# Splitting the first load of an add-GELU kernel by partitions: 16 rows first, then 112

## The chip, the cores and the metric

The kernel runs on one core of one Trainium2 chip. The metric is the device time of one execution in microseconds (us), taken as the median of several runs. "Span" is the length of a profiled execution; it is some 1.8 us shorter than the device time of the same run.

Some words: an *issue* is the instruction by which SyncE asks for a transfer. The core's 16 DMA engines carry the transfer as *packets*, each one row of a load or store, 8 to 32 KB in these two kernels. A transfer has *landed* when the last engine has signalled it. In the views DVE is VectorE, ACT is ScalarE, POOL is GpSimd and SP or SPq is SyncE.

## The reference

```python
# x, y: float32 [1024, 4096]
z = x + y
out = 0.5 * z * (1 + tanh(sqrt(2 / pi) * (z + 0.044715 * z ** 3)))   # float32
```

Two arrays of 16.8 MB come in and one goes out: 50.33 MB in all, for a handful of elementwise operations.

## The kernel before

Every array is seen as 128 partitions of 32768 elements; partition p holds eight neighbouring rows of 4096. x and y come in five column pieces each, the sum is made in place in the tile `z`, and `z` is stored again in five pieces. All loads and stores go through one queue (SyncE). The first two loads are moved ahead of the opening barrier.

```python
YS = 8192; CH = 1024; PS = 4
loads  = [2048, 6144, 8192, 8192, 8192]      # columns per partition
stores = [8192, 8192, 8192, 4096, 4096]
...
def load_x(i):
    a, b = lr[i]
    nc.sync.dma_start(out=zt[:, a:b], in_=xv[:, a:b])

def load_y(i):
    a, b = lr[i]
    s, o = divmod(a, YS)
    if o == 0:
        yt[s] = pool_y.tile([P, YS], fp32, tag="y", name=f"y{s}")     # two buffers
    nc.sync.dma_start(out=yt[s][:, o : o + b - a], in_=yv[:, a:b])
...
# per piece of 1024 columns: add (GpSimd; VectorE for the first), Square (ScalarE),
# scalar_tensor_tensor (VectorE), Sigmoid (ScalarE), multiply (VectorE)
...
sp = []
for i in range(len(loads)):
    sp += [(load_x, i), (load_y, i)]
sp += [(store, i) for i in range(len(stores))]
...
begin_early(nc, 2)      # the first two loads are issued ahead of the opening barrier
```

Of the kernel before, what the change touches and what calls it, by code (L numbers as in the profile page):

```python
# [1 line left out]

# [1 line left out]

# [4 lines left out]


def begin_early(nc, count):


    blocks = nc.main_func.blocks
    head, body = blocks[0], blocks[1]
    SP = mybir.EngineType.SP
    queue = [i for i in body.instructions if i.engine == SP]
    moved = [i for i in queue if isinstance(i, mybir.InstDMACopy)][:count]
    assert not any(i.sync_info and i.sync_info.on_wait for i in moved)
    at = next(k for k, i in enumerate(head.instructions) if i.engine == SP and isinstance(i, mybir.InstDrain))  # L20
    for k, i in enumerate(moved):
        body.instructions.remove(i)
        head.instructions.insert(at + k, i)


@with_exitstack
def kernel(
    ctx: ExitStack,
    tc: tile.TileContext,
    x: bass.AP,  # L30
    y: bass.AP,
    out: bass.AP,
):








    nc = tc.nc
    P = nc.NUM_PARTITIONS
    fp32 = mybir.dt.float32
    act = mybir.ActivationFunctionType
    alu = mybir.AluOpType

    N, D = x.shape
    assert N % P == 0
    TOT = N // P * D  # L50
    xv, yv, ov = (a.rearrange("(p n) d -> p (n d)", p=P) for a in (x, y, out))

    c1 = 2.0 * math.sqrt(2.0 / math.pi)
    root = math.sqrt(c1 * 0.044715)

    YS = 8192
    CH = 1024
    PS = 4
    loads = [2048, 6144, 8192, 8192, 8192]
    stores = [8192, 8192, 8192, 4096, 4096]  # L60

    def ranges(sizes):
        ends = [sum(sizes[: i + 1]) for i in range(len(sizes))]
        assert ends[-1] == TOT
        return [(e - f, e) for e, f in zip(ends, sizes)]

    lr, sr, cr = ranges(loads), ranges(stores), ranges([CH] * (TOT // CH))
    C = len(cr)
    by_pool = set(range(1, C))

    def over(rs, lo, hi):
        return [i for i, (a, b) in enumerate(rs) if a < hi and b > lo]

    pool_sb = ctx.enter_context(tc.tile_pool(name="xz", bufs=1))
    pool_y = ctx.enter_context(tc.tile_pool(name="y", bufs=2))
    pool_w = ctx.enter_context(
        tc.tile_pool(name="w", bufs=PS, space=bass.MemoryType.PSUM)
    )

    zt = pool_sb.tile([P, TOT], fp32, tag="z", name="z")  # L80
    yt, wt = {}, {}

    def load_x(i):
        a, b = lr[i]
        nc.sync.dma_start(out=zt[:, a:b], in_=xv[:, a:b])  # L85

    def load_y(i):
        a, b = lr[i]
        s, o = divmod(a, YS)
        if o == 0:  # L90
            yt[s] = pool_y.tile([P, YS], fp32, tag="y", name=f"y{s}")
        nc.sync.dma_start(out=yt[s][:, o : o + b - a], in_=yv[:, a:b])  # L92

    def store(i):
        a, b = sr[i]
        nc.sync.dma_start(out=ov[:, a:b], in_=zt[:, a:b])

    def add(c):
        a, b = cr[c]
        s, o = divmod(a, YS)  # L100
        eng = nc.gpsimd if c in by_pool else nc.vector
        eng.tensor_add(out=zt[:, a:b], in0=zt[:, a:b], in1=yt[s][:, o : o + b - a])  # L102

    def sq(c):
        a, b = cr[c]
        wt[c] = pool_w.tile([P, CH], fp32, tag="w", name=f"w{c}")
        nc.scalar.activation(  # L107
            out=wt[c], in_=zt[:, a:b], func=act.Square, scale=root
        )

    def stt(c):
        a, b = cr[c]
        nc.vector.scalar_tensor_tensor(  # L113
            out=wt[c], in0=wt[c], scalar=c1, in1=zt[:, a:b], op0=alu.add, op1=alu.mult
        )

    def sig(c):
        nc.scalar.activation(out=wt[c], in_=wt[c], func=act.Sigmoid)  # L118

    def mul(c):  # L120
        a, b = cr[c]
        nc.vector.tensor_mul(out=zt[:, a:b], in0=wt[c], in1=zt[:, a:b])  # L122
# [6 lines that stand above are left out]
    pool = [(add, c) for c in range(C) if c in by_pool]  # L129
    dve, acts = [], []  # L130
    for i in range(-3, C + 1):
        if 0 <= i < C:
            dve.append((stt, i))
            acts.append((sig, i))
        if 0 <= i - 1 < C:
            dve.append((mul, i - 1))
        if 0 <= i + 3 < C and i + 3 not in by_pool:
            dve.append((add, i + 3))
        if 0 <= i + 2 < C:
            acts.append((sq, i + 2))  # L140

    needs = {
        load_x: lambda i: [],
        load_y: lambda i: [
            (add, c)
            for c in over(cr, lr[i][0] - 2 * YS, lr[i][0] - YS)
            if lr[i][0] % YS == 0
        ],
        add: lambda c: [(f, i) for i in over(lr, *cr[c]) for f in (load_x, load_y)],
        sq: lambda c: [(add, c)] + ([(mul, c - PS)] if c >= PS else []),  # L150
        stt: lambda c: [(sq, c)],
        sig: lambda c: [(stt, c)],
        mul: lambda c: [(sig, c)],
        store: lambda i: [(mul, c) for c in over(cr, *sr[i])],
    }
    queues = [sp, pool, acts, dve]
    done = set()
    with tc.manual_schedule():
        one = pool_sb.tile([P, 1], fp32, tag="one", name="one")
        nc.vector.memset(one, 0.0)  # L160
        nc.scalar.activation(out=one, in_=one, func=act.Sigmoid)  # L161
        while any(queues):
            moved = False
            for q in queues:
                while q and all(n in done for n in needs[q[0][0]](q[0][1])):
                    fn, arg = q.pop(0)
                    fn(arg)
                    done.add((fn, arg))
                    moved = True
                    if q is not sp:  # L170
                        break
            assert moved, [q[:1] for q in queues]

    ctx.close()
    tc.close()
    tc.compile()
    begin_early(nc, 2)


# [1 line left out]
_INS = ['x', 'y']  # L181
_OUTS = [((1024, 4096), 'float32')]


# [23 lines left out]
```

## Time and profile before

| | before |
|---|---|
| device time, median of the first 3 runs | 122.65 us |
| profiled span | 121.2 us |
| VectorE / ScalarE / GpSimd busy | 62% / 53% / 60% |
| share of the 16 DMA engines' time in the load and store queue | 97.8% |
| moved | 50.33 MB |

How to read it: no compute engine is near full, and the DMA engines are. The kernel is one stream of loads and stores, so the questions are when the stream starts, whether it ever slows, and when it ends. Three lines of the table of stretches (stretch, length, busy time of DVE, ACT and POOL with instruction counts, clock, DMA share, GB/s), which the argument after the prediction needs; the prediction shows more of this table:

```profile
3.00:6.00 3.00, 0.00 (x0) 0.00 (x0) 0.00 (x0) 1.00 1.00 421
6.00:9.00 3.00, 1.22 (x1) 0.27 (x1) 1.48 (x1) 1.00 1.14 489
70.00:82.00 12.00, 12.00 (x12) 9.72 (x10) 10.31 (x6) 1.00 1.00 404
```

The last line is the one to remember: in that stretch the stream runs at 404 GB/s and not at the 430 or so of its neighbours.

### The profile page before, as it was taken

What the parts mean: (1) busy time and instruction counts of PE and PEld (TensorE: products, weight loads), DVE (VectorE), ACT (ScalarE), POOL (GpSimd) and SP (SyncE); (2) the same over time, 40 slices, a digit from 0 to 9 for tenths busy, and PEclk for the clock granted to TensorE, in tenths of its full rate; (3) what the DMA queues carried; (4) which work ended last, traced back from release to release, by engine and by line L of the source; (5) the groups of instructions that cost most, each with busy time, mean ns of one, the idle gap of its engine ahead of it and who ended that gap; (6) DMA issues with size and microseconds to landing.
All of it is one profiled execution on the core that took longest, in us unless ns stands there. A gap on an engine that the chain in (4) does not pass through costs nothing.

```text
span 121.2 us, 248 instructions
## 1 busy us (share of the span) xinstructions
DVE 75.5 (62%) x66; ACT 63.8 (53%) x66; POOL 73.0 (60%) x35
## 2 busy tenths in 40 slices
DVE  0044700059999019999997999994999999400000
ACT  4016200078875047888858878874878878000000
POOL 0056000699980299999889999949999990000000
DMA  6999999999999989898989898998999999989992
GB/s 197 417 468 422 471 406 433 476 389 476 389 476 389 476 379 487 357 508 357 508 346 519 346 519 346 346 487 381 479 389 476 389 476 389 487 379 411 433 433 108
DMA packets 2162, 50.35 MB, mean 416 GB/s; under 512 B 240, under 2 KB 240, under 8 KB 240
## 3 DMA queue, kind: packets, MB, share of 16 engines
q1 hardware_dynamic: 2160, 50.33, 97.8%
q14 instruction: 2, 0.02, 0.0%
HBM read 33.55 MB, written 16.78 MB: 415 GB/s over the span
## 4 chain that ended last, share of the span: by engine, by line
DMA 49%; POOL 17%; DVE 16%; SPq 1%; ACT 1%; issue 0%; POOLq 0%
DMA y<-in_y_dram 49%; POOL z L102 17%; DVE z L122 8%; DVE w L113 8%; ACT w L107 1%; SPq L85 1%; SPq L92 1%; POOLq L102 0%
## 5 line engine op out<-in xcount | busy, mean ns | idle before, releaser
L102 POOL TENSOR_TENSOR z<-z,y 128x1024 f32<-128x1024 f32 x31 | 72.8, 2388 | 26.5 <-DMA y<-in_y_dram 26.5
L113 DVE SCALAR_TENSOR_TENSOR w<-w,z 128x1024 f32<-128x1024 f32 x32 | 39.4, 1232 | 21.4 <-ACT w L107 21.4
L107 ACT ACTIVATE w<-z 128x1024 f32<-128x1024 f32 x32 | 32.9, 1028 | 37.7 <-POOL z L102 31.7
L122 DVE TENSOR_TENSOR z<-w,z 128x1024 f32<-128x1024 f32 x32 | 38.8, 1214 | 0.0
L118 ACT ACTIVATE w<-w 128x1024 f32<-128x1024 f32 x32 | 31.4, 981 | 0.4 <-DVE w L113 0.4
L102 DVE TENSOR_TENSOR z<-z,y 128x1024 f32<-128x1024 f32 x1 | 1.2, 1224 | 6.1 <-DMA y<-in_y_dram 6.1
L161 ACT ACT_TABLE_LOAD x1 | 1.3, 1283 | 1.3 <-PEq L192 1.3
L160 DVE MEMSET one<- 128x1 f32 x1 | 0.1, 59 | 1.3 <-PEq L192 1.3
L192 POOL MEMSET const-float32-0.0<- 128x1 f32 x1 | 0.1, 99 | 0.2 <-issue 0.2
L161 ACT ACTIVATE one<-one 128x1 f32<-128x1 f32 x1 | 0.2, 203 | 0.0
L192 POOL MEMSET const-bfloat16-1.0<- 128x1 bf16 x1 | 0.1, 102 | 0.0
L192 POOL MEMSET const-uint8-127<- 128x1 uint8 x1 | 0.1, 102 | 0.0
L192 POOL MEMSET const-float32-1.0<- 128x1 f32 x1 | 0.1, 99 | 0.0
## 6 DMA issues: line engine op xcount, KB each, us to landing
z<-in_x_dram SPq DMA_DIRECT2D x3, 4096.0 KB, 34.2
y<-in_y_dram SPq DMA_DIRECT2D x3, 4096.0 KB, 24.8
out_dram<-z SPq DMA_DIRECT2D x3, 4096.0 KB, 30.8
out_dram<-z SPq DMA_DIRECT2D x2, 2048.0 KB, 17.5
z<-in_x_dram SPq DMA_DIRECT2D x1, 3072.0 KB, 13.4
y<-in_y_dram SPq DMA_DIRECT2D x1, 3072.0 KB, 20.4
z<-in_x_dram SPq DMA_DIRECT2D x1, 1024.0 KB, 4.9
y<-in_y_dram SPq DMA_DIRECT2D x1, 1024.0 KB, 6.9
```

Of the source, the lines that this page charges most:

```text
L85: nc.sync.dma_start(out=zt[:, a:b], in_=xv[:, a:b])
L92: nc.sync.dma_start(out=yt[s][:, o : o + b - a], in_=yv[:, a:b])
L102: eng.tensor_add(out=zt[:, a:b], in0=zt[:, a:b], in1=yt[s][:, o : o + b - a])
L107: nc.scalar.activation(out=wt[c], in_=zt[:, a:b], func=act.Square, scale=root)
L113: nc.vector.scalar_tensor_tensor(out=wt[c], in0=wt[c], scalar=c1, in1=zt[:, a:b], op0=alu.add, op1=alu.mult)
L118: nc.scalar.activation(out=wt[c], in_=wt[c], func=act.Sigmoid)
L122: nc.vector.tensor_mul(out=zt[:, a:b], in0=wt[c], in1=zt[:, a:b])
L160: nc.vector.memset(one, 0.0)
L161: nc.scalar.activation(out=one, in_=one, func=act.Sigmoid)
L192: nc = _bacc.Bacc("TRN2", target_bir_lowering=False, num_devices=1)
```

## The change

The intent, as I read the edit, is that a small first load gets its data moving earlier, while the rest of the first megabyte follows right behind.

```diff
     def load_x(i):
         a, b = lr[i]
-        nc.sync.dma_start(out=zt[:, a:b], in_=xv[:, a:b])
+        cut = [0, 16, P] if i == 0 else [0, P]
+        for f, e in zip(cut, cut[1:]):
+            nc.sync.dma_start(out=zt[f:e, a:b], in_=xv[f:e, a:b])
 ...
-    begin_early(nc, 2)
+    begin_early(nc, 3)
```

## The prediction

The forecast's sum stands as it was made: 0.01 us for the semaphore packets, -0.15 for an earlier start, and two terms of +0.3, one for a slow load of 16 rows and one for slow packets in the load of 112 rows. That is +0.46 us, weighed down by hand to about +0.3, so 122.95 us. Where the two terms of +0.3 came from is cut. So are rivals 2 and 3, in which the cut by rows costs more, or much more, than the sum has; their chances (45% and 7%) stand in the text.

> **What bounds the kernel now.** I read four views in this order: the page's busy shares and slices, to see which resource is never idle; the table of stretches, to see when that resource starts and stops; the timeline of the first microseconds, because that is where the change sits; and the page's DMA issues with the DMA queue's waits, to see whether the transfers ever run dry later.
>
> The page first (part 1, the DMA rows of part 2, part 3):
>
> ```profile
> DVE 75.5 (62%) x66; ACT 63.8 (53%) x66; POOL 73.0 (60%) x35
> ...
> DMA  6999999999999989898989898998999999989992
> GB/s 197 417 468 422 471 406 433 476 389 476 389 476 389 476 379 487 357 508 357 508 346 519 346 519 346 346 487 381 479 389 476 389 476 389 487 379 411 433 433 108
> ...
> q1 hardware_dynamic: 2160, 50.33, 97.8%
> ```
>
> No compute engine is busy above 62%, while the 16 DMA engines are at eight or nine tenths in every slice but the first and the last, and their one hardware queue takes 97.8% of their time. The kernel is a single stream of 50.33 MB (two inputs in, one output out). Only the first slice (6) and the last (2) are not full.
>
> The table of stretches puts numbers on it. The columns are the stretch, its length, the busy time of DVE, ACT and POOL with their instructions, the TensorE clock, the DMA share and GB/s:
>
> ```profile
> 0.00:1.00 1.00, 0.00 (x0) 0.00 (x0) 0.20 (x4) 1.00 0.00 0
> 1.00:2.00 1.00, 0.06 (x1) 0.74 (x1) 0.00 (x0) 1.00 1.07 156
> 2.00:3.00 1.00, 0.00 (x0) 0.74 (x2) 0.00 (x0) 1.00 0.93 393
> 2.00:60.00 58.00, 33.74 (x30) 28.97 (x31) 35.73 (x15) 1.00 1.01 432
> 60.00:119.00 59.00, 41.72 (x37) 34.05 (x35) 37.08 (x17) 1.00 1.00 426
> ```
>
> For 1.0 us nothing moves; for the next the engines count as busy but deliver 156 GB/s; from 2.0 to 119.0 us they run at 426 to 432 GB/s. The span of 121.2 us is thus about 2.0 (start) + 117.2 (stream) + 2.0 (last write, its landing and the end). A transfer of 1 MB costs 2.4 us of stream at 432 GB/s, and what shifts the stream's first full packet shifts the end by the same amount.
>
> The timeline of the start:
>
> ```profile
> 0.00 0.38 SPq L85 DMA_DIRECT2D z<-in_x_dram  x1
> ...
> 0.43 0.42 SPq L92 DMA_DIRECT2D y<-in_y_dram  x1
> 1.26 1.28 ACT L161 ACT_TABLE_LOAD   x1 [1.26 <-PEq L192]
> 1.26 0.33 SPq L85 DMA_DIRECT2D z<-in_x_dram  x1
> ```
>
> The first issue takes 0.38 us and starts at zero. The packet records of the trace have the first 8192-byte packet at 1.01 us, so 0.63 us after that issue ended; the 16 engines take up their first packet between 1.01 and 1.41 us. Joining packets end to start, I get 16 clean chains. Thirteen engines hold their first packet for 0.89 to 1.25 us; the other three do two packets in that time. All 16 reach the steady 0.306 us per 8192 bytes (26.8 GB/s an engine) between 2.0 and 2.4 us. So about 0.7 us per engine is a cold start. By the same chains the engines write their last packets' semaphores between 118.95 and 119.52 us, except one at 119.88: two 8 KB instruction fetches (at 83.9 and 86.5 us, 0.309 us each) went through the engines as well, and I take it that this one did them. So the end follows one engine's phase, not the mean.
>
> Last, the queue:
>
> ```profile
> z<-in_x_dram SPq DMA_DIRECT2D x1, 1024.0 KB, 4.9
> y<-in_y_dram SPq DMA_DIRECT2D x1, 1024.0 KB, 6.9
> ```
>
> The first x lands at 4.9 us, the first y 6.9 us after its own issue at 0.43; the third load is issued at 1.26, long before the engines need it. The issue times and landings further on never leave the queue empty: the last store is issued at 104.4 us while the one before it lands at 115.4. The page's chain that ended last (DMA 49%, POOL 17%, DVE 16%) follows semaphores into the compute engines, but these are 11 us ahead at the end; I set it aside.
>
> [...]
>
> **The change part by part.** It removes one 128-row load of 1 MB and adds a 16-row load (128 KB) and a 112-row load (896 KB) of the same bytes, all before the opening barrier; nothing moves on DVE, ACT or POOL (their instruction lists have the same order and count).
>
> Extra issue: one more of about 0.4 us (rows of 0.38 and 0.42). The first y is issued near 0.85 instead of 0.43, still over 3 us before its packets are due at about 4.3. The barrier and the third load move from 1.26 to at most 1.7; packets of that load are due near 6.8. Table load (1.28 us) and first compute (7.48) have more slack still. On the path: 0.
>
> Extra semaphore packets: one per engine, 9 ns in the records. On the path: +0.01 us.
>
> Earlier start: if the issue's time follows its descriptors, a 16-row issue ends before 0.38 and the first packets come that much earlier. Issues of 1, 3 and 4 MB, with the same row count, take 0.33 to 0.66 us, so bytes hardly matter and rows are untried. My estimate is a gain of 0.0 to 0.3 us, middle 0.15.
>
> [...]
>
> Sum: 0.01 - 0.15 + 0.3 + 0.3[...] gives about +0.3 us: 122.65 + 0.3 = 122.95.
>
> **The rivals.** (1) Earlier start wins[...]: 122.3 to 122.6. For it: the cold start wastes 0.7 us per engine with an idle queue ahead. Against: the first packets end at 2.0 to 2.4 us whether they began at 1.01 or 1.41[...]. [...] (4) It is hidden: since the stream is bound from 2.0 us on, nothing changes: 122.6 to 122.7.
>
> **Range and chances.** Rivals 1 and 4 together some 45%, 2 some 45%, 3 some 7%. That puts the middle at 122.95, and 8 in 10 between 122.2 and 124.4. Slower by over 2% is above 125.1: rival 3 with the far edge of 2, 0.08. Faster by over 2% needs 2.45 us less, more than the whole start: 0.01. Within 2%: 0.91.
>
> **What would show it.** First packet's start: under 1.0 us proves the earlier start. [...] I am wrong altogether if the stream later has gaps, or if either part runs on fewer than 16 engines.

## The result, and the profile after

The changed kernel took 123.13 us (median of 6 runs, 123.03 to 123.39), the kernel before 122.67 us in the same rounds (6 runs, 122.49 to 123.08). The ratio is 1.0038 with a 95% interval of 1.0019 to 1.0057: slower by 0.4%, and within 2%. Ratios here are the mean time of one kernel's fast runs over the mean of the other's fast runs of the same rounds, so they differ a little from the ratio of the medians.

The SyncE timeline of the changed kernel, start (columns: start and duration in us, engine, line, what):

```profile
0.00 0.86 SPq L88 DMA_DIRECT2D z<-in_x_dram  x2
0.90 0.43 SPq L95 DMA_DIRECT2D y<-in_y_dram  x1
1.74 0.35 SPq L88 DMA_DIRECT2D z<-in_x_dram  x1
```

The two halves of the first x are one merged line here; the records behind it have the 16-row issue at 0.00 for 0.39 us and the 112-row issue from 0.445 for 0.42 us. So the small issue was no shorter than the 128-row one (0.38 us), and the bulk of the data was asked for 0.445 us later. The first packet started at 1.03 us (1.01 before).

The changed kernel's DMA issues (KB each, us from issue to landing):

```profile
y<-in_y_dram SPq DMA_DIRECT2D x1, 1024.0 KB, 7.4
z<-in_x_dram SPq DMA_DIRECT2D x1, 896.0 KB, 5.6
z<-in_x_dram SPq DMA_DIRECT2D x1, 128.0 KB, 3.0
```

The small load landed 3.0 us after its issue. The 896 KB needed 5.6 us from its own issue, more than the 4.9 us that the whole megabyte took before.

The changed kernel's table of stretches, with the same columns as before:

```profile
1.00:2.00 1.00, 0.06 (x1) 0.27 (x1) 0.00 (x0) 1.00 1.26 246
2.00:3.00 1.00, 0.00 (x0) 1.00 (x1) 0.00 (x0) 1.00 0.65 238
3.00:6.00 3.00, 0.00 (x0) 0.22 (x2) 0.00 (x0) 1.00 0.98 322
6.00:9.00 3.00, 0.55 (x1) 0.00 (x0) 0.51 (x1) 1.00 1.13 478
70.00:82.00 12.00, 12.00 (x11) 10.16 (x11) 11.04 (x6) 1.00 1.02 437
```

Against before: up to 3 us the engines had moved 484 KB (246 + 238) instead of 549 KB (156 + 393). That is 65 KB, or 0.15 us at 432 GB/s. From 3 to 6 us they ran at 322 instead of 421 GB/s: 99 GB/s for 3 us is 297 KB, or 0.69 us. From 6 to 9 us another 0.08 us (489 against 478). Together 0.92 us. And then, at 70 to 82 us, the changed kernel was *faster*: 437 against 404 GB/s, which is 33 x 12 = 396 KB, or 0.92 us. That the two figures are equal is luck: this view counts every packet whole, so the edges of a stretch are uncertain, most of all at 70 and 82 us, where each engine carries 32 KB packets. With each packet's bytes spread over its time, the records give 404 and 432 GB/s there, or 0.76 us.

How the delay runs through the kernel is seen where GpSimd begins on a newly landed y. GpSimd's timeline, before:

```profile
60.99 18.52 POOL L102 TENSOR_TENSOR z<-z,y 128x1024 f32<-128x1024 f32 x8 [0.93 <-DMA y<-in_y_dram]
81.20 4.65 POOL L102 TENSOR_TENSOR z<-z,y 128x1024 f32<-128x1024 f32 x2 [1.69 <-DMA y<-in_y_dram]
```

and after:

```profile
61.86 18.54 POOL L105 TENSOR_TENSOR z<-z,y 128x1024 f32<-128x1024 f32 x8 [0.85 <-DMA y<-in_y_dram]
81.36 4.65 POOL L105 TENSOR_TENSOR z<-z,y 128x1024 f32<-128x1024 f32 x2 [0.96 <-DMA y<-in_y_dram]
```

At the last y but one the changed kernel is 0.87 us late, at the last y only 0.16 us. VectorE's first sum, before and after:

```profile
7.48 1.22 DVE L102 TENSOR_TENSOR z<-z,y 128x1024 f32<-128x1024 f32 x1 [6.08 <-DMA y<-in_y_dram]
8.45 1.23 DVE L105 TENSOR_TENSOR z<-z,y 128x1024 f32<-128x1024 f32 x1 [6.59 <-DMA y<-in_y_dram]
```

It starts 0.97 us late. So a delay of nearly 1 us is made in the first 9 us, carried for 50 us to within 0.1 us, and then mostly lost, because something holds up the kernel *before* near 77 us and does not hold up the changed one.

### The profile page after: what moved, and what is told of

It reads as the page before. It is cut to its first block, busy times and chain, and to the rows that moved or that the text cites. A ratio compares the mean times of both kernels' runs of the same rounds, so it can differ in the third digit from the quotient of the medians.

```text
span 121.2 us, 249 instructions
## 1 busy us (share of the span) xinstructions
DVE 75.6 (62%) x66; ACT 63.8 (53%) x66; POOL 73.1 (60%) x35
## 4 chain that ended last, share of the span: by engine, by line
DMA 49%; DVE 16%; POOL 16%; issue 2%; SPq 1%; ACT 1%; POOLq 0%
DMA y<-in_y_dram 49%; POOL z L105 16%; DVE z L125 8%; DVE w L116 8%; ACT w L110 1%; SPq L88 1%; SPq L95 1%; POOLq L105 0%
## 6 DMA issues: line engine op xcount, KB each, us to landing
y<-in_y_dram SPq DMA_DIRECT2D x3, 4096.0 KB, 24.8
```

## The experiments

Twelve runs were made, two of them of the same two kernels again, and all gave right results. "Late" below is the start of the first sum on VectorE, which waits for the first x and y: 7.48 us in the first profile of before. Passages of the expectations are cut as well, and marked, where they named a cause that no run shows. What stands right behind a cut, with no theory named, was expected if a cut by rows by itself makes a load slow, unless the text here says otherwise.

### Both kernels again

No edit. The aim was to learn which of the two differences above return.

> The kernel before, unchanged, to see how much two of its profiles differ. The profile of before holds a single stall in which packets took up to 0.54 us per 8 KB between 75 and 80 us (0.78 us per engine); the profile of after has none. Theory A (the stall is a chance event): the time ratio is 1.000 within 0.2%, and this profile has no such stall or has it elsewhere; then all landings of y4 are near 80.3 us instead of 81.06. Theory B (the stall belongs to the kernel before): it is there again at 75 to 80 us.

> The changed kernel again. Ratio to before 1.003 to 1.006 in both theories. If the start alone decides (loss seen in the profile at the landing of the first y: 8.33 against 7.38 us, 0.95 us), the whole loss must reach the end: about +0.9 us without a stall in before, so 1.007. If the stall is a chance event that the changed kernel has as well in other runs, the mean difference stays under that, near 0.5 us (1.004).

Measured: before again 122.54 us (ratio to its own rounds 1.0001, interval 0.9986 to 1.0016); after again 123.20 us against 122.59 us, ratio 1.0053 (1.0038 to 1.0068). Both profiles repeat. The first, of before:

```profile
3.00:6.00 3.00, 0.00 (x0) 0.00 (x0) 0.00 (x0) 1.00 1.02 429
70.00:82.00 12.00, 12.00 (x12) 9.71 (x10) 10.18 (x6) 1.00 0.98 393
```

and the second, of after:

```profile
3.00:6.00 3.00, 0.00 (x0) 0.22 (x2) 0.00 (x0) 1.00 1.00 309
70.00:82.00 12.00, 12.00 (x12) 10.16 (x12) 11.05 (x6) 1.00 1.00 429
```

The slow start (309 against 429 GB/s from 3 to 6 us) is again the changed kernel's, and the slow stretch at 70 to 82 us (393 against 429) is again the old one's. In this pair the first sum is 1.32 us late (8.60 against 7.28). The stall belongs to before in both profiles, and to after in none. Two profiles of each are few, but the table of all 14 profiles further down sorts by kernel too, eight with the stall and six without, so the chance theory falls.

### The same bytes, cut by columns

```diff
-        nc.sync.dma_start(out=zt[:, a:b], in_=xv[:, a:b])
+        cut = [0, 256, 2048] if i == 0 else [0, b - a]
+        for f, e in zip(cut, cut[1:]):
+            nc.sync.dma_start(out=zt[:, a + f : a + e], in_=xv[:, a + f : a + e])
...
-    begin_early(nc, 2)
+    begin_early(nc, 3)
```

> Same number of loads and the same bytes in the first one (128 KB), but cut by columns: 128 partitions x 256 elements, then 128 x 1792. [...]nothing is lost, packets of the second part take the usual time for their 7 KB (0.27 us), the first y lands at 7.3 to 7.5 us, time within 0.1 us of before. Extra-issue theory (what costs is one more issue of 0.39 + 0.05 us ahead of the bulk of the data, or the second part's cold start): the first y lands 0.4 to 0.9 us later than 7.38 as in after, time +0.3 to +0.5 us.

Measured: 122.84 us against 122.59 us, ratio 1.0026 (1.0001 to 1.0051). The table of stretches:

```profile
1.00:2.00 1.00, 0.06 (x1) 0.27 (x1) 0.00 (x0) 1.00 1.17 245
2.00:3.00 1.00, 0.00 (x0) 1.00 (x1) 0.00 (x0) 1.00 0.72 251
3.00:6.00 3.00, 0.00 (x0) 0.21 (x2) 0.00 (x0) 1.00 1.02 427
```

From 2 to 3 us this kernel is as slow as the changed one (251 and 238 GB/s): that part does not depend on how the load is cut. From 3 to 6 us it is as fast as before (427). The first sum starts at 7.65 us, 0.17 to 0.37 us late. So each of the two theories, slow rows and the extra issue, holds one share of the loss: some 0.2 to 0.3 us belong to a small piece issued ahead of the bulk, and the rest, the slow stretch from 3 to 6 us, belongs to the cut by rows. Within the first share, the later issue of the bulk and a slow start of the second piece are not told apart. One more issue is not enough by itself: the needless load further down also puts one ahead of the first x, but of 0.5 MB, and loses nothing by 3 us (188 + 381 = 569 KB against 549 of before):

```profile
1.00:2.00 1.00, 0.06 (x1) 0.28 (x1) 0.00 (x0) 1.00 0.90 188
2.00:3.00 1.00, 0.00 (x0) 1.00 (x1) 0.00 (x0) 1.00 0.98 381
```

The first share of the column cut is near the noise of this run (one of its six runs took 123.58 us).

### The 16/112 cut in the middle of the stream, and its control

The same cut on the third x (4 MB), some 20 us behind the start; and that same load cut by columns.

```diff
-        nc.sync.dma_start(out=zt[:, a:b], in_=xv[:, a:b])
+        cut = [0, 16, 128] if i == 2 else [0, P]
+        for f, e in zip(cut, cut[1:]):
+            nc.sync.dma_start(out=zt[f:e, a:b], in_=xv[f:e, a:b])
```

```diff
-        nc.sync.dma_start(out=zt[:, a:b], in_=xv[:, a:b])
+        cut = [0, 1024, 8192] if i == 2 else [0, b - a]
+        for f, e in zip(cut, cut[1:]):
+            nc.sync.dma_start(out=zt[:, a + f : a + e], in_=xv[:, a + f : a + e])
```

> The first loads are whole again; instead the third load of x (4 MB, in the middle of the stream, no cold start) is cut into 16 and 112 partitions. [...]the loss of the change's load times four, since rows are 32 KB and not 8[...]; I expect +2 to +8 us (1.02 to 1.07). [...]Extra-issue or cold-start theory: no loss, under 0.05 us.

> Control to the 16/112 split of the 4 MB load in the middle: the same load is cut by columns at full width, 128 x 1024 and 128 x 7168 (the same 512 KB first). [...]+0.0 us, within 0.2%, and packets at 0.304 us per 8 KB between 20 and 42 us. If an additional load as such costs: +1 us or more.

Measured: rows 131.44 us (ratio 1.0726, 1.0705 to 1.0746), 8.85 us more; columns 122.41 us (0.9983, 0.9967 to 1.0000). The stretch 25 to 42 us, in which most of the 112-row part runs, first with rows, then with columns:

```profile
25.00:42.00 17.00, 13.90 (x12) 11.66 (x12) 11.74 (x6) 1.00 0.96 260
```

```profile
25.00:42.00 17.00, 13.91 (x12) 11.25 (x12) 11.39 (x6) 1.00 1.01 435
```

The same number of loads and the same bytes: 260 against 435 GB/s. The cut by rows cost 8.85 us, the cut by columns nothing. (The stretch takes in some full-width packets behind the 112 rows; those rows alone hold each engine for 14.9 us in the packet records, which is 245 GB/s.) The 8.85 us are a little over the 2 to 8 us that I expected. In the packet records all 16 engines slow down alike, to 1.8 to 2.7 us for a 32 KB row, against 1.215 us for a row of a full-width load.

### Sixteen rows at a time

```diff
-        nc.sync.dma_start(out=zt[:, a:b], in_=xv[:, a:b])
+        cut = [0, 16, 32, 48, 64, 80, 96, 112, 128] if i == 2 else [0, P]
+        for f, e in zip(cut, cut[1:]):
+            nc.sync.dma_start(out=zt[f:e, a:b], in_=xv[f:e, a:b])
```

> The 4 MB load of the middle as eight loads of 16 partitions each, to measure the rate of a 16-row load by itself. [...]the 4.19 MB take 38.8 us instead of 9.7, so +29 us, if loads queue strictly[...]. [...]+0.1 us.

The first figure takes 16 rows to run at a quarter of the stream's rate, which was an assumption of mine; the second is for rows that do not matter.

Measured: 147.41 us (one run), 24.8 us more. The table of stretches:

```profile
26.00:52.00 26.00, 13.91 (x12) 11.57 (x12) 11.44 (x5) 1.00 1.01 122
```

Eight loads of 16 neighbouring rows in a row run at 122 GB/s, steadily, with all 16 engines counted as busy. A 32 KB packet takes 4.30 us on its engine, so each 8 KB takes 1.075 us instead of 0.304. 4.19 MB at 122 GB/s are 34.4 us instead of 9.7, so 24.7 us more; the time shows 24.8.

Now the middle split can be added up. 0.52 MB at 122 GB/s take 4.3 us and 3.67 MB at 260 GB/s take 14.1 us, 18.4 us in all instead of 9.7: +8.7, measured +8.85. The sum fits the time a little too well: where GpSimd begins on the last y but one, this kernel is 9.6 us late (70.62 against 60.99), and at the last y 8.9 (90.10 against 81.20), because it has no stall either. A quarter of 8.7 to 9.6, for rows of 8 KB, is 2.2 to 2.4 us: by this estimate that is what the changed kernel's cut would cost with nothing to hide it.

What makes such rows slow is not shown. I had put it down to the side of the on-chip memory, which was an assumption. But every cut by rows here also changes which rows of x or y in DRAM the 16 engines read at the same time, and no run separates the two sides.

### The 16/112 cut on the first y, and a 64/64 cut on the first x

The first tells whether the start hides a part: here the cut rows come when the stream already runs.

```diff
-        nc.sync.dma_start(out=yt[s][:, o : o + b - a], in_=yv[:, a:b])
+        cut = [0, 16, 128] if i == 0 else [0, P]
+        for f, e in zip(cut, cut[1:]):
+            nc.sync.dma_start(out=yt[s][f:e, o : o + b - a], in_=yv[f:e, a:b])
...
-    begin_early(nc, 2)
+    begin_early(nc, 3)
```

The second halves the first x:

```diff
-        nc.sync.dma_start(out=zt[:, a:b], in_=xv[:, a:b])
+        cut = [0, 64, 128] if i == 0 else [0, P]
+        for f, e in zip(cut, cut[1:]):
+            nc.sync.dma_start(out=zt[f:e, a:b], in_=xv[f:e, a:b])
...
-    begin_early(nc, 2)
+    begin_early(nc, 3)
```

> The first x is whole again; the first y (1 MB) is cut into 16 and 112 partitions[...]. From the runs so far: 16 rows of 8 KB take 1.075 us on each engine (the eightfold run) instead of 0.306, so +0.77; seven rows each at the 1.7-fold pace of the middle split, 7 x 0.306 x 0.7 = +1.5. [...]first y lands 1.5 to 2.3 us later than in before (7.2 to 7.4 us), more than the 1.1 us of the changed kernel. Theory that the cold start and the late bulk issue make the loss: under 0.3 us. Second question, the stall at 77 us: if any uneven split of rows removes it (descriptor counts or order of the engines), it is absent and the end is +0.9 to +1.7 us; if it is there, +1.5 to +2.3 us.

> The first x cut into 64 and 64 partitions. [...]eight rows 4.3 us instead of 2.45, +1.9 us, of which the cold start hides some 0.3 to 0.5: first y lands 1.3 to 1.7 us later than in before. [...]0.1 to 0.2 us as with the cut by columns.

In the text on the halves, the first figures are for slow rows, with a time per row that was my estimate, and the last is for rows that do not matter.

Measured: the cut y 123.98 us (ratio 1.0117, 1.0103 to 1.0132), 1.5 us more; the halves 124.51 us (1.0159, 1.0143 to 1.0174), 2.0 us more. VectorE's first sum, first with the cut y, then with the halves:

```profile
9.75 1.22 DVE L104 TENSOR_TENSOR z<-z,y 128x1024 f32<-128x1024 f32 x1 [7.90 <-DMA y<-in_y_dram]
```

```profile
10.05 1.23 DVE L104 TENSOR_TENSOR z<-z,y 128x1024 f32<-128x1024 f32 x1 [7.70 <-DMA y<-in_y_dram]
```

With the cut y the first sum is 2.3 to 2.5 us late: the 2.2 to 2.4 us of the sum above, unhidden, and a little more than I expected at most. With the changed kernel it is 1.0 to 1.3 us, though that holds the 0.2 to 0.3 us of the small first piece too. The cut on the very first load thus costs half or less of what it costs one load later; that the cold start hides the rest is my reading. The halves are 2.6 to 2.8 us late, well over the 1.3 to 1.7 us that I expected. In the records the rounds of their packets take 0.54 to 0.63 us per 8 KB from 2.5 to 6.4 us, instead of 0.31, near the 0.54 us a row to which the expected 4.3 us come, and make some 2.0 us. But hardly any of it was hidden, and the first packet started 0.31 us later, at 1.32 instead of 1.01 us. The first three issues of that profile took 0.55, 0.58 and 0.59 us instead of 0.38 to 0.43, the one of the whole y among them, so this need not come from the 64 rows; there is one profile only.

In both profiles the stall at 77 us is absent, and the end is 0.6 to 1.0 us less late than the first sum.

### What is the cold start?

```diff
-    begin_early(nc, 2)
+    begin_early(nc, 7)
```

> The kernel before with all seven loads that wait for nothing issued ahead of the opening barrier (two before). Question: every profile has a dead stretch between about 1.5 and 2.2 us (in the changed kernel until 2.4 to 2.9) in which hardly a packet ends. If it comes from what the other engines do after the barrier (table load at 1.26 us; 1.73 in the changed kernel), it moves to about 3.5 us or vanishes. If it comes from the second or third issue or from the first large load itself, it stays at 1.5 to 2.2 us. Time within 0.3 us of before either way.

Measured: 122.68 us, ratio 0.9996 (0.9976 to 1.0016). The barrier's work moved (first line: the table load), and the dead stretch did not (second line, of its table of stretches; 156 and 205 GB/s in the two profiles of before):

```profile
4.01 1.28 ACT L161 ACT_TABLE_LOAD   x1 [4.01 <-PEq L192]
```

```profile
1.00:2.00 1.00, 0.00 (x0) 0.00 (x0) 0.00 (x0) 1.00 1.02 197
```

So the slow second microsecond does not come from the other engines' work after the barrier. What it is stays open. It isn't simply the first use of the queue: in the changed kernel the 16 small packets pass in 0.31 to 0.56 us each, and then the first packets of the 112-row load are held for 0.6 to 1.25 us.

### What is the stall at 77 us?

Three tries. A needless load of 0.5 MB ahead of everything makes the stream later without a cut by rows:

```diff
+    pad = pool_sb.tile([P, 1024], fp32, tag="pad", name="pad")
...
+        if i == 0:
+            nc.sync.dma_start(out=pad, in_=xv[:, a : a + 1024])
...
-    begin_early(nc, 2)
+    begin_early(nc, 3)
```

> The kernel before, with an unneeded whole-width load of 0.5 MB (128 x 1024, into a tile of its own) put ahead of the first x. It delays all later data by 1.21 us (0.5 MB at 432 GB/s)[...]. Question: the three profiles of kernels close to before hold a stall of all engines near 77 us (0.8 us per engine), the two of the changed kernel do not. Theory S1 (a stream that is about 1 us later misses the stall): no stall at 77 us, and the time is only +0.3 to +0.7 us. Theory S2 (the stall depends on something else): the stall is there, and the time is +1.2 to +1.4 us.

Elementwise pieces of twice the length change the rhythm of the compute engines:

```diff
-    CH = 1024
-    PS = 4
+    CH = 2048
+    PS = 2
```

> The kernel before with elementwise pieces of 2048 instead of 1024 elements and two work buffers instead of four: half the instructions, same loads and stores. It tests the step of the prediction that says one DMA engine, which also fetches two 8 KB blocks of instructions at 84 to 87 us, ends last (120.26 against 119.88 us for the next) and sets the end. If right, no fetch falls into the stream, the last store's 16 landings lie within 0.6 us, and the time is 0.2 to 0.5 us less than before. If wrong, same time within 0.1 us. The stall at 77 us is also worth a look: if it comes from the compute instructions' rhythm, it changes or goes.

And a cut by rows of 64 KB only, in the middle of the stream, should do away with the stall at little cost, if a cut by rows as such does it:

```diff
-        nc.sync.dma_start(out=zt[:, a:b], in_=xv[:, a:b])
+        parts = [(0, P, 0, b - a)]
+        if i == 2:
+            parts = [(0, 16, 0, 128), (16, P, 0, 128), (0, P, 128, b - a)]
+        for f, e, g, h in parts:
+            nc.sync.dma_start(out=zt[f:e, a + g : a + h], in_=xv[f:e, a + g : a + h])
```

> All seven profiles of kernels whose loads are all full width hold the stall at 77 to 79 us (0.34 to 0.86 us per engine), all five looked at with some load cut into rows hold none. Here only 64 KB in the middle of the stream are cut into 16 and 112 rows (the first 128 columns of the third x); the rest of that load is full width. [...]64 KB at 122 GB/s at worst is 0.54 us instead of 0.15, by the middle split's pace 0.2 us. Theory R (a row-cut load as such does away with the stall): no stall in the profile, and the time is 0.2 to 0.6 us under before, better than both kernels. Theory Q (the stall vanishes only when the stream is held up by about 1 us or more, or by chance): stall present, time 0.0 to 0.4 us above before.

Measured: the needless load 123.76 us, 1.17 us more (ratio 1.0098, 1.0078 to 1.0119); the long pieces 135.41 us (1.1050, 1.1034 to 1.1066); the small cut 122.52 us against 122.49 us (1.0001, 0.9987 to 1.0014). The long pieces are a failed experiment for the time: with two work buffers VectorE waits 44.6 us for ScalarE (21.4 before) and the stores 64.6 us for VectorE (42.2 before), so it says nothing on the instruction fetches. Their loads, though, ran as before until 81 us (the 4 MB loads of x and y landed 34.6 and 25.3 us after their issue in the median, 34.2 and 24.8 before), so they still bear on the stall. What the packet records hold between 70 and 84 us, in 32 KB packets that normally take 1.215 us (the last two kernels have the same part of their stream later, and have no such packets there either, two instruction fetches aside):

| kernel | packets over 1.25 us | excess per engine |
|---|---|---|
| before, first and second profile | 17, 27 | 0.78, 0.85 us |
| seven early issues | 28 | 0.62 us |
| columns first, columns in the middle | 23, 28 | 0.86, 0.43 us |
| needless load (stall at 78.9 us) | 19 | 0.34 us |
| long pieces | 28 | 0.65 us |
| small cut by rows | 21 | 0.32 us |
| after, first and second profile | 0, 0 | 0.01, 0.01 us |
| cut y, halves, rows in the middle, sixteen rows at a time | 0, 0, 0, 0 | 0.02 to 0.03 us |

The long pieces show that the compute rhythm does not make the stall. The needless load shows that a late stream alone does not take it away, though it is smaller there. The small cut shows that a cut by rows alone does not take it away either: theory R falls, and with it the version that I hoped would beat both kernels. What the five kernels without it share is a large cut by rows that held all 16 engines up by about 1 us or more. The records also show where the stall sits: in all eight profiles that have it, almost all slow packets are among the last two that each engine carries of the last load, right before the packets of the first store (76.8 to 79.8 us in seven profiles; in the needless load from 78.84 us on, 1.9 us later, as its stream is). In the other six profiles the same packets took 1.21 to 1.22 us in the median. So the stall belongs to the turn from loads to stores and not to a time. Why a large cut by rows helps there, and what the stall is, stays open; so does whether runs without a profile have it, though the time differences speak for it: the start costs 1.0 to 1.3 us and the runs differ by only 0.46 to 0.66 us.

## Why the prediction was right or wrong

The time (123.13 us) lies inside the range of 122.2 to 124.4 and 0.18 us over the stated 122.95. By its own steps:

- **The bound.** Right: the stream decides, and a delay made in the first microseconds was carried for 50 us to within 0.1 us, and the needless load, 1.21 us of stream by the estimate, made the time 1.17 us longer.
- **The extra issue, "on the path: 0".** Wrong by 0.2 to 0.3 us. The issue was sized right (0.39 + 0.05 us), and the first y and the barrier moved as told (0.90 and 1.74 us), but I looked only at what comes *after* the first x. The small piece and its issue stand ahead of the bulk of the first x itself, and the cut by columns, which has no slow stretch from 3 to 6 us, shows that cost alone.
- **The earlier start, gain 0.15 us.** Wrong: gain zero. The 16-row issue took 0.39 us against 0.38, and the first packet came at 1.03 us against 1.01. The issue of 16 rows took as long as that of 128.
- **The first term of +0.3, for the load of 16 rows.** That loads of 16 rows are slow is shown (122 GB/s, eight in a row); the cause is not. The term was too large: by 3 us the changed kernel had moved 484 KB and the column cut, which has no such rows, 496 KB, so 12 KB or 0.03 us instead of 0.3. The sign that I named for it, how long the first packets are held, was misjudged too. They were held only 0.31 to 0.56 us. All were over by 1.77 us, while their landings came from 2.21 to 2.99 us, so the hold of a first packet did not show how slowly such a load lands.
- **The second term of +0.3, for the 112 rows.** Right in direction, and the effect came whole and a little larger: 0.69 us in the first pair of profiles, 429 - 309 = 120 GB/s for 3 us or 0.83 us in the second, so over twice what the sum has. From 2 to 7 us the changed kernel ran at 326 GB/s in the mean (330 with each packet's bytes spread over its time, against 413 before). Its packets took 0.37 to 0.47 us between 3 and 5.5 us, against 0.31 before. The rival at 7%, a loss far over 2%, fell with the time itself; 260 GB/s for the 112 rows in the middle of the stream are also well over the 122 that 16 rows show.
- **"Wrong altogether if the stream later has gaps."** It had one, in the kernel before, and I had its sign in my own first fence: the GB/s row has two neighbouring slices at 346, where the others alternate about the mean. I read the table's 426 GB/s after 60 us as "full"; it could not have told me, since the changed kernel, which has no stall, reads 427 in the same stretch of that view. Without that stall in before, the start's 1.0 to 1.3 us might have come through; the sum of the prediction came near the time partly because a loss larger than its +0.3 us was partly given back by a thing that it did not know. That is luck.
- **The end follows the engine that fetches instructions.** Not tested: the experiment for it failed for another reason.

## What to carry to other kernels

Cut a load by columns and keep all 128 partitions: in the middle of the stream such a cut was free (122.41 us, ratio 0.9983), while 112 rows ran at about 250 GB/s and loads of 16 rows at 122 instead of 435. A smaller first load did not start sooner (first packet at 1.03 us against 1.01), as its issue took as long as a large one (0.39 us against 0.38), and it put the bulk behind one more issue, 0.445 us later. When a known delay fails to reach the end, look for a stretch in the *old* profile that was slower than its neighbours: a row of mean rates hides 0.8 us easily.
